# An fp32 kernel with TensorE busy throughout: transposes as pairs of 64-row tiles, and HGRN level scores as 32- and 64-column tiles

## The chip, the cores and the metric

The kernel runs on one core of one Trainium2 chip. The metric is the device time of one execution in microseconds (us). Every time below is in us unless it says ns. The core has five engines that matter here: TensorE (PE; its weight loads are listed apart as PEld), VectorE (DVE), ScalarE (ACT), GpSimd (POOL) and SyncE (SP, which only issues DMAs in this kernel).

## The reference

One inference step of a one-layer hybrid streaming encoder, on a prompt of 512 frames and on a sample of 32 frames that continues running streams. Two branches work in parallel on one projection and are merged by sigmoid gates.

```python
D_MODEL, SEQ, DEC_SEQ, CHUNK = 1024, 512, 32, 64
proj = xn @ w_in                      # u, v_m, z_m, ig, fg, q_h, f_h, i_h, g_h, ga, gb
# branch 1, mLSTM, 4 heads of 512: conv + silu -> q, k; chunked scores; matrix memory C
s = einsum('bhtd,bhsd->bhts', q, k) * dmat
num = w_inter * einsum('bhed,bhtd->bhte', C, q) + einsum('bhts,bhse->bhte', s, v)
# branch 2, HGRN2, 8 heads of 128
g = cumsum(lf)                                         # log forget gates
dec = exp(where(causal, g[t] - g[s], -inf))            # one decay per channel
a = einsum('bhtc,bhtsc,bhsc->bhts', q, dec, k)
o = einsum('bhtc,bhce->bhte', q * exp(g), S) + einsum('bhts,bhse->bhte', a, v)
# head norms, silu gates, y = sigmoid(ga) * ya + sigmoid(gb) * yb, two more projections, final norm
```

The outputs are both streams' frames and both branches' new states.

## The kernel before, in words

All data is held with channels on the 128 partitions and the 544 frames (32 of the sample, then 512 of the prompt) along the free dimension. The big projections are matmuls of 272 columns (names `d`, `q`, `k`, `ya`, `yb`), each in three passes, because an fp32 number is split into a high and a low part of the type fp32r. Pairs of projections (class `Two`) are made from seven products instead of eight, in half units of six passes of 272 columns.

TensorE's order is written out by hand. The list of half units is held by `Pump`; the small work of a branch is a Python generator (`mchain(h, pump)` for mLSTM head h, `chain(h)` for HGRN head h) that says `yield n` where n half units of projections are to be put between two of its steps. On TensorE the two are thus woven together: a few small matmuls, then six to eighteen projection passes, and so on. ACT, DVE and POOL are ordered by a scheduler from priorities, except in the first stage.

The change touches these places:

- Transposes. A `PE.transpose` takes a 128x128 fp32 block as weights and an identity (or `anti`, the reversed identity) of 128 columns as the moving operand. `paux` gives a PSUM tile of two banks. `mchain` transposes keys (`kt`, four blocks per 128 frames, L1122; `kts` for the sample, 96 columns, L1135), values (`vt` L1157, `vts` L1175, heads 1 to 3) and the normed outputs (`yt` L1307, four blocks and one of the sample, L1308). `chain` transposes `kq` to sum a diagonal (`pd`, five blocks, L1871), values and keys (`ht`, five blocks each, L1902 and L1903) and outputs (`hoT`, five blocks, L1975 and L1976).
- HGRN scores. `chain(h)` builds the causal scores of a 128-frame block from seven levels c = 1, 2, 4, ..., 64 (`LEVELS`): at level c the keys of one half of each 2c frames meet the queries of the other half. Per level ACT copies keys into `km` (L1818), TensorE multiplies `km` with `qq`, two 128x128 fp32 products into `pl` (L1832, each in two passes), DVE copies what the level needs into `at` under a mask (`COPY_PREDICATED`, L1857), and DVE multiplies `kk` and `qq` by the level's decays (L1850), after which the next `km` can be copied. At c = 16 two more products serve the sample (L1834, L1836), one of them from `snap`, the sample's keys and queries of four levels side by side.
- Sample products. `su` (states, L1922) and `ho` (outputs, L1948 and L1949) have the sample's 32 frames held as four copies in 128 rows.

Of the kernel before, what the change touches and what calls it, by code (L numbers as in the profile page):

```python
# [17 lines left out]
P = 128  # L18
D = 1024
KD = D // P  # L20
NS = 32
# [15 lines left out]
QUADS = P // NS  # L37
STEPS = (2, 3, 3, 3, 3, 3, 3)
# [29 lines left out]
def hybrid_step(ctx: ExitStack, tc: tile.TileContext, a, o):  # L68
# [45 lines left out]
    def psplit(src, name, ring):  # L114
        hi, lo = pair_tile(name, ring)
        S.copy(hi, src)
        V.tensor_tensor(lo, src, hi.bitcast(F32), ALU.subtract)
        return hi, lo

# [196 lines left out]
    def masks():  # L316

        t = cp.tile([P, T], F32, tag="lm", name="lmask")
        u, n = t[:, :T].bitcast(U8), len(LEVELS) * HB
        return u[:, :n].rearrange("p (l t) -> p l t", l=len(LEVELS)), u[:, n : n + NS]  # L320
# [791 lines left out]
    def mchain(h, pump):  # L1112
# [5 lines left out]
        for b in range(NB):  # L1118
            yield 4 if h else 1
            pt = paux(f"kt{h}{b}")  # L1120
            for f in range(KH):
                PE.transpose(pt[:, 0, f * P : (f + 1) * P], kf[f][:, NS + b * P : NS + (b + 1) * P], ident)  # L1122
            kh, kl = slot(f"kwh{h}{b}", F32R), slot(f"kwl{h}{b}", F32R)
            wc = col[:, 10 + b, h : h + 1]
            with tc.high_priority():
                kh_ = S.mul(kh[:, :HD], pt[:, 0, :], wc)
                kl_ = V.scalar_tensor_tensor(kl[:, :HD], pt[:, 0, :], wc, kh[:, :HD].bitcast(F32), ALU.mult, ALU.subtract)
            kw.append((kh, kl))
            if h == 0 and b == NB - 2:
                with tc.issue_after(kh_.ins), tc.issue_after(kl_.ins):  # L1130
                    sample_values(vsum)
        yield 4 if h else 2
        pt = paux(f"kts{h}")
        for f in range(KH):
            PE.transpose(pt[: 3 * NS, 0, f * P : (f + 1) * P], ksm[:, f], ident)  # L1135
# [3 lines left out]
        with tc.high_priority():  # L1139
            S.mul(kws, pt[: 3 * NS, 0, :], wc)  # L1140
            lo = slice(2 * NS, 3 * NS)
            low = V.scalar_tensor_tensor(kws[lo], pt[lo, 0, :], wc[lo], kws[lo].bitcast(F32), ALU.mult, ALU.subtract)
# [6 lines left out]
        else:  # L1149
# [3 lines left out]
            for b in range(NB):  # L1153
                yield 1
                pt = paux(f"vt{h}{b}")
                for f in range(KH):
                    PE.transpose(pt[:, 0, f * P : (f + 1) * P], vt[f][:, NS + b * P : NS + (b + 1) * P], ident)  # L1157
# [5 lines left out]
                with tc.high_priority():  # L1163
                    S.copy(vh[:, :HD], pt[:, 0, :])
                    V.tensor_tensor(vl[:, :HD], pt[:, 0, :], vh[:, :HD].bitcast(F32), ALU.subtract)
# [8 lines left out]
            for f in range(KH):  # L1174
                PE.transpose(pt[: 3 * NS, 0, f * P : (f + 1) * P], vsm[:, f], ident)  # L1175
            vs = small("vs", [3 * NS, VW], F32R, bufs=1)
            with tc.high_priority():
                S.copy(vs[:, :HD], pt[: 3 * NS, 0, :])
            G.tensor_copy(vs[:, HD:VW], vone)
            lo = slice(NS, 2 * NS)  # L1180
            with tc.high_priority():
                low = V.tensor_tensor(vs[lo, :HD], pt[lo, 0, :], vs[lo, :HD].bitcast(F32), ALU.subtract)
# [116 lines left out]
        for f in range(KH):  # L1299
# [6 lines left out]
            for b in range(NB):  # L1306
                PE.transpose(pt[:, 0, b * P : (b + 1) * P], yb[b][:, f * P : (f + 1) * P], ident)  # L1307
            PE.transpose(pt[:, 1, :P], yb[NB][:, f * P : (f + 1) * P], ident)  # L1308
# [4 lines left out]
            with tc.high_priority():  # L1313
                V.scalar_tensor_tensor(c[:, NS:T], pt[:, 0, :], g, c[:, NS:T], ALU.mult, ALU.add)
                V.scalar_tensor_tensor(c[:, :NS], pt[:, 1, :NS], g, c[:, :NS], ALU.mult, ALU.add)
# [65 lines left out]
    def level_masks():  # L1381
        lmask, smask = masks()
        sxt = small("sxt", [P, P + 2 * NS], bufs=1, tag="vsm")
        nc.sync.dma_start(sxt, a["sxt"])
        for i, c in enumerate(LEVELS):
            V.tensor_scalar(
                lmask[:, i, : 2 * P].rearrange("p (b t) -> p b t", b=2),
                sxt[:, :P].rearrange("p (o t) -> p o t", o=1).to_broadcast([P, 2, P]),
                float(c),
                None,  # L1390
                ALU.is_ge,
            )
        V.tensor_scalar(smask, sxt[:, P : P + NS], 0.5, None, ALU.is_ge)
        V.tensor_scalar(lmask[:, QUADS, 2 * P :], sxt[:, P + NS :], 0.5, None, ALU.is_ge)
        return lmask, smask
# [227 lines left out]
    with tc.manual_schedule(engines={mybir.EngineType.PE}):  # L1623
        for h in range(MH):
# [46 lines left out]
            if h == 0:  # L1671
                with tc.issue_after(last.ins):
                    next(bounds)
                    lmask, smask = level_masks()
# [21 lines left out]
    def units():  # L1696
# [49 lines left out]
        def gate(h, t):  # L1746
            sg = slot(f"sg{h}")
            S.activation(sg[:, :T], t[:, :T], AF.Sigmoid)
            V.tensor_tensor(t[:, :T], t[:, :T], sg[:, :T], ALU.mult)
# [51 lines left out]
    def chain(h):  # L1801

        tf, kk, q0, qq, kq, ii = (hs[h][k] for k in ("tf", "kk", "q0", "qq", "kq", "ii"))
        at = tp.tile([P, NA + P], F32, tag="bc", name=f"at{h}")
        G.memset(at, 0.0)
        snap = small("snap", [P, 2, QUADS, NS], bufs=1, tag="ksm")
# [5 lines left out]
        for li, c in enumerate(LEVELS):  # L1812
            smp = li == QUADS
            n = HB if smp else NA
            km = tp.tile([P, NA], F32, tag="vs", name=f"km{h}{c}", bufs=1)
            pump.behind = held[-1] if held else None
            with tc.high_priority():
# [4 lines left out]
                if li < QUADS:  # L1822
                    S.copy(snap[:, :, li], hs[h]["pair"][:, :, csmp])
# [3 lines left out]
            pn = paux(f"pl{h}{c}")  # L1827
            for b in range(2):
                out, dims = pn[:, 0, b * P : (b + 1) * P], ((2 * c, P // (2 * c)), (HB + c, 2), (1, c))
                if c == 1:  # L1830
                    out, dims = out.rearrange("p (i s) -> p s i", s=2), (dims[1], dims[0])
                PE.matmul(out, km[:, b * P : (b + 1) * P], view(qq, b * P, dims), start=True, stop=True)  # L1832
# [8 lines left out]
            with tc.high_priority():  # L1841
# [15 lines left out]
                V.copy_predicated(at[:, :n], lmask[:, li, :n], pn[:, 0, :n])  # L1857
                if smp:
                    for i in range(QUADS):
                        d = slice(i * NS, (i + 1) * NS)  # L1860
                        V.copy_predicated(at[d, NA:HB], smask[d], pn[d, 1, d])
# [4 lines left out]
            if li == 0:  # L1866
# [3 lines left out]
                for b, c_ in enumerate([c_ for c_, _, _ in chunks] + [slice(NA, NA + P)]):  # L1870
                    PE.transpose(pn[:, b // NB, b % NB * P : (b % NB + 1) * P], kq[:, c_], ident)  # L1871
                with tc.high_priority():
                    V.tensor_reduce(
                        dg, pn.rearrange("p a t -> p (a t)")[:, : 5 * P].rearrange("p (b t) -> p b t", t=P), AX.X, ALU.add
                    )
# [11 lines left out]
        def quads(src, i):  # L1887
            G.tensor_copy(snap[:, i], src[:, csmp].rearrange("p (o t) -> p o t", o=1).to_broadcast([P, QUADS, NS]))
            return snap[:, i].rearrange("p l t -> p (l t)")

        kt, it = kk[:, :NP], ii[:, :NP]
        ov = kq
        osb = small("osb", [P, P])
        kit = small("kit", [P, 2, P], tag="qw")
# [3 lines left out]
        for n, src, dst, dss in ((0, ii, it, its), (2, kk, kt, kts)):  # L1898
            yield n
            pt = paux(f"ht{h}")  # L1900
            for b, (c, _, _) in enumerate(chunks):
                PE.transpose(pt[:, 0, b * P : (b + 1) * P], src[:, c], ident)  # L1902
            PE.transpose(pt[:, 1, :P], quads(src, n // 2), ident)  # L1903
            with tc.high_priority():
                S.copy(dst, pt[:, 0, :])
                if n:
                    S.mul(dss, pt[:, 1, :P], 1.0 / QUADS)
                else:
                    S.copy(dss, pt[:, 1, :P])
            if n == 0:  # L1910
# [3 lines left out]
                S.mul(osb, its, dg[:, 4:5])  # L1914
# [33 lines left out]
        PE.matmul(po[:, 1, :P], at[:, NA:], its, start=True, stop=False)  # L1948
        PE.matmul(po[:, 1, :P], qq[:, NA : NA + P], s0, start=False, stop=True)  # L1949
        with tc.high_priority():  # L1950
            V.tensor_tensor(ov[:, :NP], po[:, 0, :], ov[:, :NP], ALU.add)  # L1951
            V.tensor_tensor(osb, po[:, 1, :P], osb, ALU.add)
        hv, hr = small("hv", [P, 5]), small("hr", [P, 5])
        osq = small("osq", [P, P], bufs=1, tag="vsm")
        for b in range(NB):
            S.activation(osq, ov[:, b * P : (b + 1) * P], AF.Square, accum_out=hv[:, b : b + 1])  # L1956
        S.activation(osq, osb, AF.Square, accum_out=hv[:, NB : NB + 1])
# [9 lines left out]
        V.tensor_scalar(osb, osb, hr[:, NB : NB + 1], None, ALU.mult)  # L1967
        hs[h].update(ov=ov, osb=osb)

    def finish(h):  # L1970
# [3 lines left out]
        for b, (_, _, j) in enumerate(chunks):  # L1974
            PE.transpose(pt[:, 0, b * P : (b + 1) * P], ov[:, b * P : (b + 1) * P], ident if j else anti)  # L1975
        PE.transpose(pt[:, 1, :P], osb, anti)  # L1976
        g = vcol(V_HG + h)
        ob = slot(f"ob{h}")
        V.scalar_tensor_tensor(ob[:, NS:T], pt[:, 0, :], g, gg[:, NS:T], ALU.mult, ALU.mult)
        V.scalar_tensor_tensor(ob[:, :NS], pt[:, 1, P - NS : P], g, gg[:, :NS], ALU.mult, ALU.mult)  # L1980
# [231 lines left out]
def _sxt():  # L2212

    p, t = np.arange(P)[:, None], np.arange(P)[None, :]
    s, q, u = p % NS, p // NS, t[:, :NS]
    band = (s > u) & ((s ^ u) >> q == 1)
    last = (p < NS) & (p > u) & ((p ^ u) >= NS // 2)
    return np.concatenate([p ^ t, band, last], axis=1).astype(np.float32)
# [76 lines left out]
```

## Time and profile before

| | |
|---|---|
| runs | 1103.76, 1104.29, 1106.26 us; median 1104.29 |
| profiled execution, first to last instruction | 1101.5 us |
| PE busy | 1092.4 us, 99%, 8625 passes |
| DVE busy | 922.8 us, 84% |
| ACT busy | 693.1 us, 63% |
| POOL busy | 209.5 us, 19% |
| HGRN stage (627 to 885 us): PE, DVE, ACT busy | 257.33, 248.00, 183.14 of 258 us |

The profiled execution's own total time is not among the times shown; its span lies 2.8 us below the median of the runs, and the rest lies before the first and after the last instruction. In a timeline row the columns are the start, the time that the group's records cover, the engine, the line, the operation, out<-in by the program's names, the weights' rows*columns, the moving operand's shape and the count. A matmul's recorded length holds its latency; what it costs on a full TensorE is the distance from its start to the next one's.

### The profile page before, as it was taken

To read this page: it belongs to the slowest core of one execution; us is meant where nothing else is said; L and a number is where in the kernel's file an instruction comes from. 1 tells how busy PE (TensorE), PEld (TensorE's weight loads), DVE (VectorE), ACT (ScalarE), POOL (GpSimd) and SP (SyncE) were. 2 spreads that over 40 slices of the span, in tenths; PEclk is the share of its full clock that TensorE was granted. 3 is DMA by queue.
4 is the path that set the end of the run, shared out by engine and by line. 5 is a ranking of instruction groups with operands and counts; after the bars stand their busy time and mean duration, and the time that the engine had idled before them with its cause. 6 is when DMAs were issued, how large, how long until landed. Compare 5 with 4: busy or idle time off the path is not lost.

```text
span 1101.5 us, 23773 instructions
## 1 busy us (share of the span) xinstructions
PE 1092.4 (99%) x8625; PEld 1070.9 (97%) x8625; DVE 922.8 (84%) x2103; ACT 693.1 (63%) x1579; POOL 209.5 (19%) x375
## 2 busy tenths in 40 slices
PE   9999999999999999999999999999999999999997
PEld 9899999999999999999999999999999999999997
DVE  7889988686896786986888799999999977778885
ACT  7777557754666554665656476776776666446683
POOL 5204010303022021202120123232232210000002
PEclk9999999999999999999999999999999999999999
DMA  7135415639355276554798665666765683337753
GB/s 241 50 124 157 156 58 185 158 125 220 119 178 179 93 178 176 164 167 146 212 261 254 172 145 141 144 135 152 159 145 150 155 222 103 110 90 242 247 180 121
DMA packets 97262, 176.58 MB, mean 160 GB/s; under 512 B 11284, under 2 KB 18580, under 8 KB 96888
## 3 DMA queue, kind: packets, MB, share of 16 engines
q1 hardware_dynamic: 81072, 141.01, 39.9%
q0 software_dynamic: 15184, 32.93, 16.2%
q8 instruction: 68, 1.11, 0.4%
q10 hardware_dynamic: 888, 1.12, 0.3%
q14 instruction: 50, 0.41, 0.1%
HBM read 150.10 MB, written 41.69 MB: 174 GB/s over the span
## 4 chain that ended last, share of the span: by engine, by line
PE 93%; DMA 3%; DVE 2%; issue 1%; SPq 0%; ACT 0%; POOL 0%; ACTq 0%; POOLq 0%
PE d L608 44%; PE ya L167 9%; PE yb L167 4%; PE q L167 4%; PE k L167 4%; PE C L1077 4%; PE nm L1257 3%; PE sc L1037 2%; PE pl L1832 2%; PE u L291 2%; PE d L460 2%; PE vp L1576 2%; DMA ws<-in_w_in 1%; PE ple L167 1%; PE kt L1122 1%; PE ht L1902 1%
## 5 line engine op out<-in xcount | busy, mean ns | idle before, releaser
L495 POOL DMA_DIRECT2D ws<-in_w_in x46 | 40.2, 875 | 211.3 <-DVE hkq L1850 32.2
L622 ACT COPY t<-d 128x272 f32<-128x272 f32 x153 | 58.0, 379 | 14.0 <-PE d L608 14.0
L1850 DVE TENSOR_TENSOR hkq<-hkq,q 128x288 f32<-128x288 f32 (+1 forms) x96 | 40.7, 431 | 2.6 <-PE pl L1834 1.0
L785 DVE SCALAR_TENSOR_TENSOR cv<-ub,vec,cv 128x547 f32<-128x547 f32 x48 | 37.6, 784 | 1.6 <-ACT cv L780 1.2
L1832 PE MATMUL pl<-hkq,km 128*128 128x128 f32 x224 | 36.2, 283 | 0.6 <-ACT km L1818 0.5
L1818 ACT COPY km<-hkq 128x256 f32<-128x256 f32 x56 | 23.9, 428 | 14.2 <-DVE hkq L1850 5.2
L1832 PEld LDWEIGHTS pl<-hkq,km 128*128 128x128 f32 x224 | 30.3, 189 | 2.0 <-ACT km L1818 1.5
L1191 DVE SCALAR_TENSOR_TENSOR c<-c,wi,Cs 128x258 f32<-128x258 f32 x32 | 15.3, 479 | 18.8 <-PE Cs L1189 18.5
L1354 DVE TENSOR_TENSOR y<-ya,y 128x272 f32<-128x272 f32 x48 | 18.9, 435 | 12.1 <-PE ya L167 10.3
L1089 ACT COPY Co<-C 128x258 f32<-128x258 f32 x30 | 9.8, 378 | 27.3 <-PE C L1077 24.9
L1857 DVE COPY_PREDICATED at<-lmask,pl 128x256 f32<-128x256 uint8 (+1 forms) x56 | 25.2, 451 | 0.1
L777 POOL COPY uo<-ub 128x3 f32<-128x3 f32 x16 | 18.7, 1167 | 34.5 <-DVE ub L631 26.6
L1268 ACT COPY y<-nm 128x516 f32<-128x516 f32 x16 | 9.4, 590 | 23.0 <-PE nm L1257 22.5
L133 POOL TENSOR_TENSOR wple50l<-wple5r,wple50h 128x256 fp32r<-128x256 f32 x1 | 0.7, 736 | 120.9 <-ACT wple50h L132 120.9
L961 POOL COPY ksm<-kf 128x96 f32<-128x96 f32 x16 | 7.1, 445 | 84.9 <-ACT kf L975 84.9
L961 POOL COPY vsm<-vt 128x96 f32<-128x96 f32 x12 | 6.3, 525 | 85.9 <-ACT vt L633 43.5
L1797 POOL TENSOR_SCALAR_AFFINE_SELECT aa<-at 128x128 f32<-128x128 f32 x32 | 19.6, 643 | 8.2 <-DVE at L1857 8.0
L581 POOL DMA_DIRECT2D ws<-in_w_in x14 | 14.6, 1043 | 33.1 <-DVE ws272l L133 27.3
L1245 DVE BATCH_NORM_STATS2 bs<-y 128x6 f32<-128x512 f32 (+1 forms) x20 | 13.8, 692 | 8.3 <-ACT y L1268 8.0
L1257 PE MATMUL nm<-vhl,sh 128*128 128x258 f32 x112 | 18.4, 286 | 0.0
L376 POOL DMA_DIRECT2D w_pg_d<-in_w_pg x16 | 13.1, 818 | 25.1 <-issue 21.4
L1956 ACT ACTIVATE osq<-kq 128x128 f32<-128x128 f32 x32 | 9.8, 305 | 12.4 <-DVE kq L1951 12.1
(4735 smaller groups left out, 5086.7 us busy)
## 6 DMA issues: line engine op xcount, KB each, us to landing
ws<-in_w_in POOLq DMA_DIRECT2D x60, 256.0 KB, 4.9
ws<-in_w_in SPq DMA_DIRECT2D x46, 256.0 KB, 3.9
ya_d<-y SPq DMA_DIRECT2D x32, 272.0 KB, 2.3
y<-ya_d SPq DMA_DIRECT2D x24, 272.0 KB, 3.3
w_out_d<-in_w_out POOLq DMA_DIRECT2D x24, 256.0 KB, 6.5
w_pg_d<-in_w_pg POOLq DMA_DIRECT2D x24, 256.0 KB, 6.5
c<-in_C SPq DMA_DIRECT2D x16, 258.0 KB, 3.8
out_Cs<-c SPq DMA_DIRECT2D x16, 258.0 KB, 3.8
```

The source lines that it names most:

```text
L167: PE.matmul(both[b][:m, :TH], part(w, off + k * step, m, x), xx[:, half(b)], start=(k == 0 and j == 0), stop=(k == n - 1 and j == 2),)
L291: PE.matmul(both[b][:m, :TH], part(w, off + k * step, m, x), xx[:, half(b)], start=(k == 0 and j == 0), stop=(k == KD - 1 and j == 2),)
L495: G.dma_start(t, piece(u, i), accum_op=ALU.add)
L608: PE.matmul(ps, ww[:, c], xx, start=(start and k == 0 and j == 0), stop=end, skip_group_check=not start,)
L622: self.kept = S.copy(t, ps)
L785: V.scalar_tensor_tensor(cv[:, :547], ub[:, j : j + 547], vcol(V_CW + 4 * ft + j), cv[:, :547], ALU.mult, ALU.add)
L1077: PE.matmul(pn[g][:, :VH], kw[b][x][:, f * P : (f + 1) * P], vv[b][y][:, g * VH : (g + 1) * VH], start=(b == 0 and j == 0), stop=(b == NB ...
L1257: PE.matmul(pn[:, g, :VH], st[j][x][:, (i - j) * P : (i - j + 1) * P], vv[j][y][:, g * VH : (g + 1) * VH], start=(j == 0 and q == 0), stop ...
L1818: low = S.copy(km.rearrange("p (n j c) -> p n j c", j=2, c=c), view(kk, HB, ((2 * c, NA // (2 * c)), (c - HB, 2), (1, c))),)
L1832: PE.matmul(out, km[:, b * P : (b + 1) * P], view(qq, b * P, dims), start=True, stop=True)
L1850: V.tensor_tensor(x, x, d, ALU.mult)
L1857: V.copy_predicated(at[:, :n], lmask[:, li, :n], pn[:, 0, :n])
```

## The change

Each transpose becomes two: rows 0 to 63 and rows 64 to 127 of the block, each with a 64-column identity, as TensorE tiles of 64 rows and 128 columns that write the two banks of the PSUM tile. What reads PSUM then reads both banks in one instruction with one more dimension, and where it is a `scalar_tensor_tensor` on `kt`, `kts` or `yt`, in two instructions. The sample's last block of `yt` and `hoT` is transposed alone, as a tile of 32 rows.

The level scores are computed only in the blocks that a level needs: for c up to 32 as eight products of 128 rows, 32 weight columns and 32 moving columns (in four column tiles that write 32 partitions each), for c = 64 as four of 64 by 64. For c below 32 four more 32x32 products compute the sample's scores at every level. The masked copy on DVE is 96 columns wide and done at five levels; c = 32 and c = 64 are copied by ACT (one copy and four small ones; two small ones). `snap` and its copies are gone. The sample's state and output products take 32 rows instead of 128.

```diff
+    def turn(pt, i, src, eye=None):
+        n = src.shape[-1]
+        for r in range(2):
+            k = slice(r * HP, (r + 1) * HP)
+            at_ = ident[k, k] if eye is None else eye[k, P - (r + 1) * HP : P - r * HP]
+            PE.transpose(pt[:n, r, i * HP : (i + 1) * HP], src[k], at_)
+    def turned(pt, n, m=P):
+        return pt[:m, :, : n * HP].rearrange("p r (f c) -> p f r c", f=n)
...
-                PE.transpose(pt[:, 0, f * P : (f + 1) * P], kf[f][:, NS + b * P : NS + (b + 1) * P], ident)
+                turn(pt, f, kf[f][:, NS + b * P : NS + (b + 1) * P])
...
-                PE.transpose(pt[:, 0, b * P : (b + 1) * P], yb[b][:, f * P : (f + 1) * P], ident)
-            PE.transpose(pt[:, 1, :P], yb[NB][:, f * P : (f + 1) * P], ident)
+                turn(pt, b, yb[b][:, f * P : (f + 1) * P])
+            PE.transpose(pt[:, 0, 2 * P : 2 * P + NS], yb[NB][:NS, f * P : (f + 1) * P], ident[:NS, :NS])
...
-                if li < QUADS:
-                    S.copy(snap[:, :, li], hs[h]["pair"][:, :, csmp])
...
+            w = max(c, NS)
             for b in range(2):
-                out, dims = pn[:, 0, b * P : (b + 1) * P], ((2 * c, P // (2 * c)), (HB + c, 2), (1, c))
...
-                PE.matmul(out, km[:, b * P : (b + 1) * P], view(qq, b * P, dims), start=True, stop=True)
-            if smp:
-                PE.matmul(pn[:, 0, NA:HB], kk[:, NA : NA + P], qq[:, csmp], start=True, stop=True)
-                ks, qs = (snap[:, i].rearrange("p l t -> p (l t)") for i in range(2))
-                PE.matmul(pn[:, 1, :P], ks, qs, start=True, stop=True)
+                for g in range(P // w):
+                    key = b * P + g * w
+                    out = pn[g * w : (g + 1) * w, 0, b * w : (b + 1) * w]
...
+                    PE.matmul(out, km[:, key : key + w], ask, start=True, stop=True)
+            if c < NS:
+                for g in range(QUADS):
+                    PE.matmul(
+                        pn[g * NS : (g + 1) * NS, 0, 2 * NS : 3 * NS], kk[:, csmp], qq[:, csmp], start=True, stop=True
+                    )
...
-                V.copy_predicated(at[:, :n], lmask[:, li, :n], pn[:, 0, :n])
...
+                if c < NS:
+                    V.copy_predicated(near, lmask[:, li], pn[:, 0, : 3 * NS])
+                elif c == NS:
+                    S.copy(far, pn[:, 0, : 2 * NS])
+                else:
+                    for g in range(2):
+                        k = slice(g * c, (g + 1) * c)
+                        S.copy(
...
+            if c == NS:
+                for g in range(QUADS):
...
+                    S.copy(at[k, :NA].rearrange("p (b q s t) -> p b q s t", b=2, q=2, s=2)[:, :, g // 2], both_)
...
-        PE.matmul(po[:, 1, :P], at[:, NA:], its, start=True, stop=False)
-        PE.matmul(po[:, 1, :P], qq[:, NA : NA + P], s0, start=False, stop=True)
+        PE.matmul(po[:NS, 1, :P], near[:NS, 2 * NS :], its, start=True, stop=False)
+        PE.matmul(po[:NS, 1, :P], qq[:, csmp], s0, start=False, stop=True)
```

TensorE's order of projections and steps stays as it was; what changes is what stands in a step. In `mchain` of head 0, first block of `yt`, TensorE has before (here `d` is a projection, `y` a normed output of 128 frames; shapes are the moving operand's, and the numbers behind the names tell tiles apart):

```order
L608 MATMUL d_2103<-xfh_1737,wa224l 128x272
L1307 MATMUL yt_2239<-ident,y_1940 128x128
L1307 MATMUL yt_2239<-ident,y_1962 128x128
L1307 MATMUL yt_2239<-ident,y_1991 128x128
L1307 MATMUL yt_2239<-ident,y_2029 128x128
L1308 MATMUL yt_2239<-ident,y_1732 128x128
L608 MATMUL d_2103<-xfh_1755,wa224h 128x272
```

and with the change, in the same place:

```order
L624 MATMUL d_2128<-xfh_1762,wa224l 128x272
L129 MATMUL yt_2264<-ident,y_1965 128x64 x2
L129 MATMUL yt_2264<-ident,y_1987 128x64 x2
L129 MATMUL yt_2264<-ident,y_2016 128x64 x2
L129 MATMUL yt_2264<-ident,y_2054 128x64 x2
L1339 MATMUL yt_2264<-ident,y_1757 128x32
L624 MATMUL d_2128<-xfh_1780,wa224h 128x272
```

Five instructions became nine between the same two projection passes. In `chain(1)` the step of level c = 64 and the transpose of the values behind it stand on TensorE before as

```order
L608 MATMUL d_9598<-xfh_1326,ws374l 128x272
L1832 MATMUL pl_9802<-hkq_8958,km_9772 128x128 x2
L1902 MATMUL ht_9818<-ident,hi_9136 128x128 x4
L1903 MATMUL ht_9818<-ident,snap 128x128
L608 MATMUL d_9836<-xh_714,wa1151h 128x272
```

and with the change as

```order
L624 MATMUL d_9921<-xfh_1326,ws374l 128x272
L1860 MATMUL pl_10163<-hkq_9194,km_10133 64x64 x4
L129 MATMUL ht_10182<-ident,hi_9393 128x64 x10
L624 MATMUL d_10204<-xh_714,wa1151h 128x272
L624 MATMUL d_10204<-xl_715,wa1151h 128x272
```

Two kinds of tile, 64 columns wide and then 64 rows high, now follow each other without a projection between them. ACT's queue ahead of the same step, from `km` of c = 32 to `km` of c = 64, reads before

```order
L1818 COPY km_9730<-hkq_8958 128x256
L1720 ACTIVATE q_9714<-hkq_9364 128x288
L1721 ACTIVATE q_9714<-hkq_9364 128x256
L132 CAST wa2274h<-wi66r_9545 128x512
L622 COPY t_9750<-d_9598 128x272
L132 CAST ws474h<-ws_9389 128x512
L1818 COPY km_9772<-hkq_8958 128x256
```

and with the change

```order
L1841 COPY km_10081<-hkq_9194 128x256
L1746 ACTIVATE q_10060<-hkq_9661 128x256
L149 CAST wa1251h<-wi51r_9825 128x512
L638 COPY t_10101<-d_9921 128x272
L149 CAST wa2274h<-wi66r_9859 128x512
L1889 COPY at_9783<-pl_10115 128x64
L1906 COPY at_9783<-at_9783 32x2x64 x4
L149 CAST ws474h<-ws_9690 128x512
L1841 COPY km_10133<-hkq_9194 128x256
```

The copies out of level 32's product (L1889) and the four that place its blocks (L1906) now stand between the two `km` copies, ahead of the one that level 64 needs.

More of the change, by code (lines that the diff above doesn't have):

```diff
@@ L1134, in mchain @@
         for f in range(KH):
[L1135 removed]
+            turn(pt, f, ksm[:, f])
         kws = small("kws", [3 * NS, HD], F32R, bufs=1)
@@ L1901, in chain @@
             for b, (c, _, _) in enumerate(chunks):
-                PE.transpose(pt[:, 0, b * P : (b + 1) * P], src[:, c], ident)
-            PE.transpose(pt[:, 1, :P], quads(src, n // 2), ident)
+                turn(pt, b, src[:, c])
+            turn(pt, NB, src[:, NA : NA + P])
             with tc.high_priority():
[L1905 to L1909, printed above, removed]
+                S.copy(quarters(dst), turned(pt, NB))
+                S.copy(two(dss), pt[:NS, :, NB * HP : (NB + 1) * HP])
             if n == 0:
```

140 lines of the change are left out of this document (77 added, 63 removed).

## The prediction

> **What bounds the kernel now.** I read the busy shares first, then TensorE's waits, then the timeline of TensorE around each kind of small step. Two lines of the page:
>
> ```profile
> PE 1092.4 (99%) x8625; PEld 1070.9 (97%) x8625; DVE 922.8 (84%) x2103; ACT 693.1 (63%) x1579; POOL 209.5 (19%) x375
> ...
> PE 93%; DMA 3%; DVE 2%; issue 1%; SPq 0%; ACT 0%; POOL 0%; ACTq 0%; POOLq 0%
> ```
>
> TensorE is busy from end to end, and 93% of the chain that ended last is its own. A busy share can hide waits, since records carry latency; but of all that it waited for after its warm-up, the list of waits has this at the top:
>
> ```profile
> PE pl L1832 <- ACT km L1818: 0.5, 1, 0.5
> ```
>
> So TensorE's time is a sum of slots, and the change is worth what it takes from or adds to those slots. DVE and ACT count only where they make TensorE late. The price of a small step is read as the distance from the last projection pass before it to the second one behind it (the first one's start is recorded early), less two projection slots. The timeline of TensorE, for slots and transposes:
>
> ```profile
> 651.50 1.05 PE L1921 MATMUL su<-hi,hkq 128*128 128x128 f32 x8
> 652.39 0.39 PE L1922 MATMUL su<-kit 128*128 128x128 f32 x2
> ...
> 250.19 0.29 PE L608 MATMUL d<-xh,wa1236l 128*128 128x272 f32 x1
> 250.32 0.60 PE L1157 MATMUL vt<-ident,vt 128*128 128x128 f32 x4
> ...
> 250.89 0.29 PE L608 MATMUL d<-xl,wa1236h 128*128 128x272 f32 x1
> ...
> 153.52 0.29 PE L608 MATMUL d<-xfh,wa224l 128*128 128x272 f32 x1
> 153.64 0.60 PE L1307 MATMUL yt<-ident,y 128*128 128x128 f32 x4
> 154.08 0.27 PE L1308 MATMUL yt<-ident,y 128*128 128x128 f32 x1
> ...
> 154.32 0.29 PE L608 MATMUL d<-xfl,wa224h 128*128 128x272 f32 x1
> ```
>
> From the last projection pass to the first start behind it go 0.13, 0.12 and, in the next fence, 0.13: a slot is 0.126. Eight fp32 passes of 128 columns take 0.89, so 0.111 each. Four transposes cost 250.89 - 250.19 - 0.25 = 0.45, five cost 0.80 - 0.25 = 0.55. The same for level steps, at c = 8, c = 16, and c = 64 with the five transposes (`ht`) that follow it:
>
> ```profile
> 637.12 0.29 PE L608 MATMUL d<-xh,wa1273l 128*128 128x272 f32 x1
> 637.25 0.64 PE L1832 MATMUL pl<-hkq,km 128*128 128x128 f32 x4
> ...
> 637.86 0.29 PE L608 MATMUL d<-xfl,wa2249h 128*128 128x272 f32 x1
> ...
> 670.59 0.29 PE L608 MATMUL d<-xh,ws450l 128*128 128x272 f32 x1
> 670.72 0.61 PE L1832 MATMUL pl<-hkq,km 128*128 128x128 f32 x4
> ...
> 671.74 0.29 PE L608 MATMUL d<-xl,ws450h 128*128 128x272 f32 x1
> ...
> 677.74 0.29 PE L608 MATMUL d<-xfh,ws374l 128*128 128x272 f32 x1
> 677.88 0.71 PE L1832 MATMUL pl<-hkq,km 128*128 128x128 f32 x4
> ...
> 679.11 0.29 PE L608 MATMUL d<-xl,wa1151h 128*128 128x272 f32 x1
> ```
>
> They cost 0.74 - 0.25 = 0.49, 1.15 - 0.25 = 0.90, and 1.37 - 0.25 = 1.12.
>
> **What the new tiles cost.** The trace of before already holds fp32 steps in smaller tiles: transposes in 32 rows (`cols`), and products in four 32-column tiles side by side (`vq`, `nm` L1203). `nm` L1204 is an fp32r product and runs like a full tile.
>
> ```profile
> 90.73 0.42 PE L167 MATMUL q<-cs3h,wq001l 128*128 128x272 f32 x2
> 91.08 1.27 PE L916 MATMUL cols<-ident,row 4*128 4x4 f32 x18
> 92.22 0.28 PE L918 MATMUL cols<-ident,r 4*96 4x4 f32 x3
> 92.43 0.52 PE L167 MATMUL q<-cs0h,wq010h 128*128 128x272 f32 x2
> 92.78 0.41 PE L167 MATMUL q<-cs0l,wq010h 128*128 128x272 f32 x2
> ...
> 46.56 0.63 PE L1576 MATMUL vp<-wv3h,x 128*128 128x512 f32 x2
> 47.03 0.40 PE L1576 MATMUL vp<-wv3l,x 128*128 128x512 f32 x1
> 47.36 0.62 PE L1586 MATMUL vq<-wv0r,xg 128*32 128x512 f32 x1
> ...
> 47.38 0.62 PE L1586 MATMUL vq<-wv3r,xg 128*32 128x512 f32 x1
> 47.81 0.59 PE L1586 MATMUL vq<-wv0r,xg 128*32 128x512 f32 x1
> ...
> 48.35 0.72 PE L1576 MATMUL vp<-wv4h,x 128*128 128x512 f32 x2
> 48.91 0.40 PE L1576 MATMUL vp<-wv4l,x 128*128 128x512 f32 x1
> ...
> 118.81 0.31 PE L1204 MATMUL nm<-vs,dss 96*32 96x258 f32 x1
> 119.05 0.64 PE L1203 MATMUL nm<-c,qw 128*32 128x258 f32 x8
> 119.62 0.30 PE L1204 MATMUL nm<-vs,dss 96*32 96x258 f32 x1
> 119.76 0.41 PE L460 MATMUL d<-xh,wi350h 128*128 128x272 f32 x2
> ```
>
> What the reader is to see is time that no column explains. `cols`: 18 passes start 0.063 apart (1.14 / 18), three more at 0.05; that is 1.28, and four slots of `q` are 0.50; 92.78 - 90.73 is 2.05, so 0.27 is left. `vq`: 48.91 - 47.03 = 1.88, less two rounds of 0.43 (47.81 - 47.38) and three `vp` slots of 0.235 (47.03 - 46.56 for two), leaves 0.32. `nm`: 119.76 - 118.81 = 0.95, less two rounds of 258 columns (0.43 x 258 / 512 = 0.22 each) and two slots of L1204 (0.126 x 258 / 272 = 0.12 each), leaves 0.27. In each case TensorE runs empty before the new kind of tile and again behind it, and the first weights cannot be loaded ahead. I take **0.30 for leaving full tiles and coming back**, with 0.27 and 0.33 as ends; and 0.12 for one more change of tile inside a step (119.05 - 118.81, less L1204's own 0.12).
>
> Within a kind of tile work does overlap: the four `vq` tiles start within 0.02, and their streams cost 0.84 ns per column (0.43 for 512), so rounds of 32, 64 and 128 columns cost 0.027, 0.054, 0.108. For a half transpose the stream is 0.054, but its weights are still 128 columns, and `cols` shows such loads 0.063 apart in one row tile. No row shows two row tiles at once. Side by side a pair costs 0.063, one after the other 0.126; I take 0.063, because the column tiles, the nearest row, run side by side.
>
> **The sum.** Groups of four transposes (16 `kt`, 4 `kts`, 12 `vt`, 3 `vts`): 0.30 + 4 x 0.063 = 0.55 against 0.45, 35 x 0.10 = +3.5. Groups of five (8 `pd`, 8 second `ht`): 0.62 against 0.55, +1.1. `yt` and `hoT` end in a 32-row tile: 0.55 + 0.12 for the change + 0.063 for the weights + 0.03 = 0.76 against 0.55, 24 x 0.21 = +5.0. Levels 1, 2, 4, 8: 8 + 4 products of two passes in four tiles are six rounds, 0.30 + 6 x 0.027 = 0.46 against 0.49, 32 x -0.03 = -1.0. Level 16: 0.46 against 0.90, 8 x -0.44 = -3.5. Level 32: four rounds, 0.41 against 0.49, -0.6. Level 64 and the first `ht` share one way out and back: 0.30 + 4 x 0.054 + 0.12 + 5 x 0.063 = 0.95 against 1.12, -1.4. `su`: two passes of 0.111 keep their length and gain a tile change, 8 x 0.30 = +2.4. `ho`: four passes of 0.111 become 0.108 each in two further kinds of tile, 0.30 + 0.12 + 0.43 = 0.85 against 0.45, +3.2.
>
> ACT: at c = 64 `km` has no slack.
>
> ```profile
> L1823 ACT COPY snap<-hkq 128x64 f32<-128x64 f32 x31 | 7.6, 245 | 0.0
> ```
>
> ```profile
> 676.42 0.62 ACT L132 CAST ws474h<-ws 128x512 fp32r<-128x512 f32 x1 [0.95 <-PE d L608]
> 677.42 0.41 ACT L1818 COPY km<-hkq 128x256 f32<-128x256 f32 x1 [0.38 <-DVE hkq L1850]
> ```
>
> It ends at 677.83, and `pl` starts at 677.88. Five copies now stand ahead of it, and they wait for level 32's product; at 0.245 (the nearest copy) they are 1.2, against 1.33 of idle time there. TensorE waits between 0 and 1.2 per chain; I take 0.2, +1.6. The rest costs nothing on TensorE's path: DVE gains 44 short instructions and loses wider masked copies, and ACT loses the `snap` copies, both beside TensorE; if that cover failed, `km` would be late, which is the term just counted. No DMA moves.
>
> The sum is +10.3 on the profiled 1101.5, and I put as much on the median of the runs, 1104.29, which lies 2.8 above that span: **1114.6**. Counted over, the change goes out of full tiles and back 147 times and changes tile 40 times more inside a step; that is 49 us of new cost (44 and 5) against 39 saved.
>
> **Rivals.** *Changing tiles is cheap for these.* If neither the 147 trips nor the 40 changes cost anything, the 49 go away: about 1066. The point from which it decides is a trip of 0.23 (10.3 / 147 = 0.07 less than 0.30). Against it stand three rows of three shapes between 0.27 and 0.33; for it, that none of them is 64 rows high. The Trainium skill (TensorEngine Tiling (Array Packing), Theoretical Speedup) promises up to 2x for a dimension up to 64 and 4x up to 32; that is this rival's rule, and by these rows it holds for the streams alone.
>
> *The two row halves run one after the other.* 356 pairs (140 + 80 + 96 + 40) cost 0.063 more: +22, 1137. For it: the only repeated half-like load, `cols`, came at 0.063 and no faster; against it, `vq`.
>
> *Every short pass has a fixed price.* At `cols`' 0.063 whatever the tile, six rounds of four become 1.5 instead of 0.16, 40 x 1.35 = +54, with the halves in turn some 1190. Against it: four starts within 0.02. The Trainium skill (TensorEngine Tiling (Array Packing), Instruction Overhead) speaks against this change here: about 60 cycles per matmul however few columns. By an estimate from it, 25 ns at the 2.4 GHz it gives elsewhere (TensorE: Matmul & The Clock Gate, Terms), a level of 24 passes would take 0.60 and the sum end near 1135; the starts in `vq` disagree.
>
> **Chances.** Forecast 0.58 (its own range 1108 to 1127: trips of 0.27 to 0.33 move it by 4.4 either way, the wait for `km` by -1.6 to +8). Halves in turn 0.18, fixed price 0.05. Cheap changes 0.13. A trip near 0.23, no change, 0.06. A measurement of this kernel can tell 0.2%, 2.2 us, from no change. So faster 0.13, same 0.06, slower 0.81; the range 1104 to 1140 leaves out the cheap changes and the fixed price.
>
> **What would show it.** In the profile after: from the last projection pass before a `kt` step to the second behind it 0.80 (0.55 + 0.25), not 0.70; the two halves of a pair starting within 0.02, pairs 0.06 apart; the c = 8 step near 0.71; the c = 16 step down to it; an idle stretch of TensorE's loads of about 0.2 ahead of each small tile. A half following the other at 0.06 shows the second rival, a step without the gap the first. It would be wrong if 64-row tiles need no emptying, or if TensorE waits for `km` far more than 0.2.

## The result, and the profile after

The changed kernel takes 1117.97 us (median of four runs, 1117.28 to 1118.82) against 1104.03: a ratio of 1.0124, with an interval of 1.0110 to 1.0138. It is 13.9 us slower; 10.3 were forecast. The profiled executions are 1117.0 and 1101.5 us long, 15.5 apart. In the runs on record a total lies 1.7 to 2.0 above its own span (1118.82 for 1117.0), so of the 2.8 between the span before and its median only about 1.8 lie outside the span. The execution profiled before was some 0.7 below its median, the one after 0.9 above its own; that makes up the difference between 15.5 and 13.9.

The page's busy shares and the chain that ended last, after:

```profile
PE 1107.4 (99%) x9877; PEld 1053.0 (94%) x9877; DVE 914.4 (82%) x2095; ACT 706.4 (63%) x1603; POOL 189.0 (17%) x367
...
PE 90%; ACT 3%; DVE 3%; issue 1%; DMA 1%; SPq 0%; ACTq 0%; DVEq 0%
```

TensorE is still busy from end to end. It issues 1252 more instructions, and its weight loads are busy for less of the span (94% for 97%). The first load of a small step does not run ahead while a projection streams: in the `kt` step below it starts at 233.34, together with its own pass and 0.22 behind the last projection pass.

The small steps, read as in the prediction: from the last projection pass before a step to the second one behind it, less 0.25. TensorE's timeline of the changed kernel, for a `kt` group, a level 4 step, level 16, level 64 with the first `ht`, `su`, and `hoT`:

```profile
233.12 0.29 PE L624 MATMUL d<-xfh,ws320l 128*128 128x272 f32 x1
233.34 0.46 PE L129 MATMUL kt<-ident,kf 64*128 64x64 f32 x8
...
233.96 0.29 PE L624 MATMUL d<-xl,wa1122h 128*128 128x272 f32 x1
...
706.54 0.28 PE L624 MATMUL d<-xh,wa1175l 128*128 128x272 f32 x1
706.75 0.33 PE L1860 MATMUL pl<-hkq,km 128*32 128x32 f32 x16
...
707.31 0.28 PE L624 MATMUL d<-xl,wa1175h 128*128 128x272 f32 x1
...
712.12 0.29 PE L624 MATMUL d<-xh,ws451l 128*128 128x272 f32 x1
712.33 0.33 PE L1860 MATMUL pl<-hkq,km 128*32 128x32 f32 x16
...
712.89 0.29 PE L624 MATMUL d<-xl,ws451h 128*128 128x272 f32 x1
...
719.10 0.29 PE L624 MATMUL d<-xfh,ws375l 128*128 128x272 f32 x1
719.54 0.45 PE L1860 MATMUL pl<-hkq,km 128*64 128x64 f32 x8
...
720.61 0.29 PE L624 MATMUL d<-xl,wa1152h 128*128 128x272 f32 x1
...
724.02 0.29 PE L624 MATMUL d<-xh,wa1252l 128*128 128x272 f32 x1
724.15 1.05 PE L1957 MATMUL su<-hi,hkq 128*128 128x128 f32 x8
725.13 0.48 PE L1958 MATMUL su<-kit 32*128 32x128 f32 x2
...
725.77 0.29 PE L624 MATMUL d<-xfl,wa2275h 128*128 128x272 f32 x1
...
744.82 0.28 PE L624 MATMUL d<-xh,ws452l 128*128 128x272 f32 x1
...
745.43 0.24 PE L2013 MATMUL hoT<-anti,osb 32*128 32x32 f32 x1
...
745.83 0.29 PE L624 MATMUL d<-xfl,ws276h 128*128 128x272 f32 x1
```

They give 0.59 for `kt`, 0.52 for both steps of levels 4 and 16, 1.26 for level 64 with `ht`, 1.50 for `su`, 0.76 for `hoT`. The first small pass starts 0.21 or 0.22 behind the last projection pass (later at level 64, of which more below), where a full tile starts 0.126 behind it. Summed over all steps of each kind, before and after:

| steps | forecast | before, us | after, us | measured |
|---|---|---|---|---|
| 35 groups of four | +3.5 | 15.9 | 20.4 | +4.5 |
| `pd`, second `ht` (16) | +1.1 | 8.8 | 10.4 | +1.6 |
| `yt`, `hoT` but the last | +5.0 | 13.1 | 19.1 | +6.0 |
| levels 1, 2, 4, 8 (32) | -1.0 | 15.5 | 16.8 | +1.2 |
| level 16 (8) | -3.5 | 7.5 | 4.2 | -3.3 |
| level 32 (8) | -0.6 | 3.9 | 3.9 | +0.1 |
| level 64, first `ht`, last `hoT`; `km` late | +0.2 | 10.2 | 10.7 | +0.5 |
| `su` (8) | +2.4 | 8.9 | 12.0 | +3.1 |
| `ho` (8) | +3.2 | 16.1 | 19.5 | +3.4 |

The sum is +17.1. The two profiled executions differ by 15.5; the 1.6 between the two stands outside the small steps. Of that, 1.2 lies behind TensorE's last pass, which ends 6.5 before the end of the span before and 5.4 after; the rest was not traced.

### The profile page after: what moved, and what is told of

It reads as the page before. It is cut to its first block, busy times and chain, and to the rows that moved or that the text cites. A ratio compares the mean times of both kernels' runs of the same rounds, so it can differ in the third digit from the quotient of the medians.

```text
span 1117.0 us, 26333 instructions
## 1 busy us (share of the span) xinstructions
PE 1107.4 (99%) x9877; PEld 1053.0 (94%) x9877; DVE 914.4 (82%) x2095; ACT 706.4 (63%) x1603; POOL 189.0 (17%) x367
## 3 DMA queue, kind: packets, MB, share of 16 engines
q8 instruction: 77, 1.26, 0.5%
q10 hardware_dynamic: 888, 1.12, 0.3%
## 4 chain that ended last, share of the span: by engine, by line
PE 90%; ACT 3%; DVE 3%; issue 1%; DMA 1%; SPq 0%; ACTq 0%; DVEq 0%
PE d L624 42%; PE ya L184 9%; PE yb L184 4%; PE q L184 4%; PE k L184 4%; PE C L1093 4%; PE nm L1288 3%; PE sc L1053 2%; PE u L308 2%; PE d L476 2%; PE vp L1601 2%; PE pl L1860 1%; PE ple L184 1%; ACT at L1906 1%; PE ht L129 1%
## 5 line engine op out<-in xcount | busy, mean ns | idle before, releaser
L638 ACT COPY t<-d 128x272 f32<-128x272 f32 x153 | 58.0, 379 | 15.9 <-PE d L624 15.5
L1860 PEld LDWEIGHTS pl<-hkq,km 128*32 128x32 f32 (+1 forms) x832 | 13.2, 112 | 10.3 <-ACT km L1841 3.5
L1860 PE MATMUL pl<-hkq,km 128*32 128x32 f32 (+1 forms) x832 | 19.7, 204 | 1.3 <-ACT km L1841 0.5
L1822 POOL TENSOR_SCALAR_AFFINE_SELECT aa<-at 128x128 f32<-128x128 f32 x32 | 16.0, 565 | 14.2 <-ACT at L1893 14.2
L392 POOL DMA_DIRECT2D w_pg_d<-in_w_pg x16 | 13.1, 819 | 25.6 <-issue 25.5
L793 POOL COPY uo<-ub 128x3 f32<-128x3 f32 x16 | 10.0, 628 | 42.8 <-DVE ub L647 29.4
L1288 PEld LDWEIGHTS nm<-vhl,sh 128*128 128x128 f32 x112 | 15.4, 190 | 0.5 <-ACT Co L1105 0.5
```

Source lines behind the costliest of these rows:

```text
L638: self.kept = S.copy(t, ps)
L1288: PE.matmul(pn[:, g, :VH], st[j][x][:, (i - j) * P : (i - j + 1) * P], vv[j][y][:, g * VH : (g + 1) * VH], start=(j == 0 and q == 0), stop ...
L1860: PE.matmul(out, km[:, key : key + w], ask, start=True, stop=True)
```

## Experiments

Differences are taken to the median of the kernel before measured beside each run, 1104.0 to 1104.7.

**The two parts alone.** First the transposes alone, in the kernel before; then their opposite, the changed kernel with full transposes in all but the sample's block of `hoT`, which stays a 32-row tile:

```diff
-    PE.transpose(pt[:, 0, f * P : (f + 1) * P], kf[f][:, ...], ident)
+    turn(pt, f, kf[f][:, ...])          # e1: every group; levels, su, ho as before
```

> The kernel before with only the transposes changed (all 91 groups in 64-row halves, the samples of `yt` and `hoT` in a 32-row tile); level scores, `su` and `ho` in full tiles as before. If the cost of the whole change is round trips at the price of the step sum, this part carries most of it: by the prediction's terms +3.5 +1.1 +5.0 = +9.6 and about +0.9 for the first `ht`, which has a trip of its own here, so 1114.5; with the steps as they stand in the profile after (0.59 for four, 0.65 for five, 0.76 with the 32-row tile) about +11.5, so 1115.5. If the cost lay in the scores (small `su` and `ho` tiles, copies ahead of `km`) and the halves were free, within 2 us of 1104.

> The changed kernel with every transpose back in full 128x128 tiles; level scores, `su` and `ho` stay in small tiles. By the step sum: levels 1 to 8 +1.4 (0.52 for 0.48), level 16 -3.0, level 32 0, level 64 alone with its late `km` +1.5, `su` +3.1, `ho` +3.4: about +6, 1110. If the cost of the change lay in the scores, 1116 or more; if the transposes carry all of it, 1104.

(The groups are 83, not 91.) Measured: 1113.5, +9.6 (ratio 1.0087, 1.0072 to 1.0102), and 1109.3, +5.3 (1.0050, 1.0035 to 1.0065). Both parts lose. Together they are 14.9 against the 13.9 of the whole, but a part of the cost of `hoT` stands in both: with four full blocks and the one 32-row tile its step is 0.81 in the second kernel, for 0.55 before, in seven chains, so 1.8 of the 5.3 belong to that tile. The steps alone have the costs that they have in the whole change: `kt` 0.59, `su` 1.50.

**The price of a trip by itself.** A trip is leaving full tiles and coming back to them. Here small tiles that nothing reads stand behind full transposes:

```diff
     # kt: behind the four full transposes
+    PE.transpose(pt[:, 1, :NS], kf[0][:NS, ...], ident[:NS, :NS])
     # vt: four such passes
```

> The kernel before with 28 added trips whose output nothing reads: one 32-row transpose behind each of the 16 `kt` groups, four behind each of the 12 `vt` groups. At the prediction's price a `kt` step becomes 0.30 + 0.06 longer and a `vt` step 0.30 + 4 x 0.063 = 0.55: 16 x 0.36 + 12 x 0.55 = +12.4, 1116.5. At a trip of 0.36 (what the halves' groups leave over their streams in the profile after) +14, 1118. If the cost of the changed kernel is in the halves or in writing two banks and not in leaving full tiles, only the passes remain: 16 x 0.06 + 12 x 0.25 = +4, 1108 or less.

Measured: 1115.8, +11.8 (1.0110, 1.0093 to 1.0127). TensorE's timeline of that kernel, a `kt` and a `vt` step:

```profile
232.13 0.29 PE L608 MATMUL d<-xfh,ws320l 128*128 128x272 f32 x1
232.25 0.60 PE L1122 MATMUL kt<-ident,kf 128*128 128x128 f32 x4
232.78 0.24 PE L1123 MATMUL kt<-ident,kf 32*128 32x32 f32 x1
...
233.19 0.29 PE L608 MATMUL d<-xl,wa1122h 128*128 128x272 f32 x1
...
405.79 0.29 PE L608 MATMUL d<-xh,wa1240l 128*128 128x272 f32 x1
...
406.44 0.43 PE L1160 MATMUL vt<-ident,vt 32*128 32x32 f32 x4
...
407.04 0.29 PE L608 MATMUL d<-xfl,ws340h 128*128 128x272 f32 x1
```

The `kt` step is 0.81, the `vt` step 1.00; both were 0.44. One pass added 0.37, four added 0.56, so a pass costs 0.06 and the way out and back 0.31. The price stands without a half or any changed reader: the forecast's 0.30 holds. The added passes do write the second bank of the PSUM tile, but so do the full tiles of `yt` in the kernel before, where a fifth transpose costs 0.11 like the others. The `hoT` step of the run above, with one 32-row pass in place of a full one, has the same 0.81. A `kt` group of eight halves leaves 0.59 - 0.31 = 0.28 for eight passes of which one alone costs 0.06: they do run in pairs.

**Halves in turn.**

```diff
-    for f in range(KH):
-        turn(pt, f, ...)                # top half, bottom half, next block
+    for r in range(2):                  # all top halves, then all bottom halves
+        for f in range(KH):
+            turn(pt, f, ..., rs=(r,))
```

> The changed kernel with the halves of a group in another order: all top halves first, then all bottom halves, so that neighbours in the order share a row tile. If a pair costs 0.058 because its two halves run side by side, each of the 356 pairs (35 groups of four, 24 of five, 24 of four) now costs 0.058 more: +20.6, 1138.6. If a half is cheap by itself (half the rows, half the load) and nothing runs side by side, no change: 1118. If the two row tiles overlap whatever the order, also 1118, with starts 0.003 apart across the two runs of four.

Measured: 1121.4, 3.4 above the changed kernel. Groups of four hardly changed (`kt` 0.60 for 0.59), groups of five did. TensorE's timeline, `pd`, of this kernel and then of the changed one:

```profile
701.33 0.28 PE L624 MATMUL d<-xfh,ws251l 128*128 128x272 f32 x1
701.54 0.65 PE L129 MATMUL pd<-ident,kq 64*128 64x64 f32 x10
...
702.35 0.29 PE L624 MATMUL d<-xfl,ws251h 128*128 128x272 f32 x1
```

```profile
700.85 0.28 PE L624 MATMUL d<-xfh,ws251l 128*128 128x272 f32 x1
701.06 0.53 PE L129 MATMUL pd<-ident,kq 64*128 64x64 f32 x10
...
701.75 0.28 PE L624 MATMUL d<-xfl,ws251h 128*128 128x272 f32 x1
```

0.77 for 0.65, twice 0.06; 24 such groups make some 2.8 of the 3.4. None of the three expectations gave this. A record does not name its half, so this is read from the starts. In a group of four the first two passes still start within 0.02 of each other, where passes of one half stand 0.06 apart; so one of them is a bottom half, with three top halves between the two in the order. In a group of five, four stand between them, and the starts are four single ones and three pairs: seven slots instead of five. That two halves side by side cost what one costs alone is shown by the difference.

**Fewer trips.**

```diff
-    yield 4 if h else 1
+    yield 0 if b % 2 else (8 if b and h else 4) if h else 1 + b // 2   # vt alike; the yields behind them too
```

> The changed kernel with the `kt` groups and the `vt` groups issued two at a time, with no projection pass between the two: 14 ways out of full tiles and back fewer (8 and 6), the same passes. If the price is paid for each leaving and coming back, 14 x 0.31 (the trip that the added passes gave) and 14 x 0.05 (the longer first pair): -5.0, 1113. If it is paid for each group (its first weights, its two banks), no change: 1118. If the readers of the first group now make the second late, something between.

Measured: 1116.0 (1.0109, 1.0094 to 1.0124), 2.0 below the changed kernel, with intervals that overlap. The steps say more. TensorE's timeline, two `kt` groups together, and the waits of TensorE on the moved groups:

```profile
236.00 0.29 PE L624 MATMUL d<-xfh,wa2220l 128*128 128x272 f32 x1
236.22 0.72 PE L129 MATMUL kt<-ident,kf 64*128 64x64 f32 x16
...
237.10 0.28 PE L624 MATMUL d<-xfl,ws222h 128*128 128x272 f32 x1
```

```profile
PE kt L129 <- DVE kwl L1145: 0.6, 2, 0.3
...
PE vt L129 <- DVE vt L645: 0.4, 1, 0.4
```

A double step is 0.85 where two single ones were 1.18: a trip saved, as expected. Over all `kt` and `vt` steps 3.3 us went, not 14 x 0.33 = 4.6, since two of the double steps waited (1.73 and 1.42 long) for a PSUM reader or for a source that was not ready so early. Even so, a double step only draws level with two full groups, 2 x 0.44.

**The second kind of tile in a step.** The expectation speaks of `yt` and `hoT`; the edit took in `yt` alone, 16 of the 24 groups, so its terms are to be read with two thirds.

```diff
-    PE.transpose(pt[:, 0, 2 * P : 2 * P + NS], yb[NB][:NS, ...], ident[:NS, :NS])
+    turn(pt, NB, yb[NB][:, ...], rs=(0,))
```

> The changed kernel with the sample rows of `yt` and `hoT` in the top 64-row half (one pass, its lower 32 rows unused) and no 32-row tile. If a second kind of tile inside a step costs 0.12 or more, a step falls from 0.76 to 0.59 + 0.06 = 0.65: 24 x 0.11 = -2.6, 1115.3. If only leaving full tiles costs, the pass costs the same in either tile: 1118.

Measured: 1117.5 (1.0123, 1.0108 to 1.0138), not to be told from the changed kernel. TensorE's timeline of a `yt` step:

```profile
158.43 0.29 PE L624 MATMUL d<-xh,ws44l 128*128 128x272 f32 x1
158.65 0.52 PE L129 MATMUL yt<-ident,y 64*128 64x64 f32 x9
...
159.33 0.29 PE L624 MATMUL d<-xl,ws44h 128*128 128x272 f32 x1
```

0.65 for 0.76, as expected; all `yt` steps together fell by 1.6 us.

**The copies ahead of `km`.** In the changed kernel ACT's timeline at level 64 reads:

```profile
717.30 1.23 ACT L1906 COPY at<-at 32x128 f32<-32x128 f32 x4
718.55 0.62 ACT L149 CAST ws475h<-ws 128x512 fp32r<-128x512 f32 x1
719.08 0.40 ACT L1841 COPY km<-hkq 128x256 f32<-128x256 f32 x1
```

`km` ends at 719.48 and `pl` starts at 719.54, 0.43 behind the last projection pass instead of 0.21. The four copies were moved:

```diff
-    S.copy(at[k, :NA].rearrange(...)[:, :, g // 2], both_)
+    G.tensor_copy(at[k, :NA].rearrange(...)[:, :, g // 2], both_)
```

> The changed kernel with the four copies that place level 32's blocks on POOL, away from ACT's row ahead of level 64's `km`. If these copies make `km` late, the step of level 64 with the first `ht` falls from 1.24 to about 1.02: 8 x 0.22 = -1.8, 1116.2. If `km` is late for another reason (DVE's product, ACT's weight casts), no change: 1118. If POOL's copies take so long that the scores are late for `triangle`, slower than 1118.

Measured: 1118.8 (1.0132, 1.0116 to 1.0149), no gain. The step did fall, from 1.24 to 1.03 in most chains, so the copies are what made `km` late; 1.3 us were won there and 1.3 lost at the second `ht` and `su` behind it. Of what was lost, this wait of TensorE is the largest:

```profile
PE su L1957 <- ACT hkq L1944: 0.7, 1, 0.7
```

**Level 16 alone: four versions.** It is the one step that gains clearly, so it was put alone into the kernel before:

```diff
+    for g in range(QUADS):              # c == 16 only; other levels in full tiles
+        d, key = slice(g * NS, (g + 1) * NS), b * P + g * NS
+        PE.matmul(pn[d, 0, key : key + NS], km[:, key : key + NS], ask, ...)
```

> The kernel before with level 16 alone in 128x32 column tiles (eight key tiles, five sample tiles, the blocks copied by nine short masked copies); every other step as before. By the price of a trip (0.31) and six to seven rounds at 0.03: a step of 0.53 for 0.89, 8 x 0.36 = -2.9, 1101.1, the one place where the saved streams pay the trip. If DVE, busy nearly throughout this stage, is made late by eight more short copies, 1104 or more.

Measured: 1122.6, 18.5 slower (1.0168, 1.0153 to 1.0183). The level 16 step did fall, to 0.56. The waits of TensorE, its timeline at level 64, and DVE's timeline there:

```profile
PE ht L1917 <- DVE at L1866: 12.8, 6, 2.1
```

```profile
677.09 0.69 PE L1838 MATMUL pl<-hkq,km 128*128 128x128 f32 x4
679.91 1.09 PE L1917 MATMUL ht<-ident,hi 128*128 128x128 f32 x4 [2.13 <-DVE at L1866]
...
681.46 0.43 PE L608 MATMUL d<-xh,wa1151l 128*128 128x272 f32 x1
681.69 0.43 PE L608 MATMUL d<-xh,wa1151h 128*128 128x272 f32 x1
```

```profile
679.33 0.43 DVE L1866 COPY_PREDICATED at<-lmask,pl 128x256 f32<-128x256 uint8 x1
...
679.87 0.25 DVE L1995 SCALAR_TENSOR_TENSOR ob<-hoT,vec,hg 128x32 f32<-128x32 f32 x1
```

DVE's row, the order of its instructions, is made by a planner from priorities. With other copies in it, the second reader of `hoT` (the 32 columns at 679.87) slid behind level 64's masked copy. In the kernel before it stood ahead of even level 32's, which DVE starts at 676.59:

```profile
675.45 0.25 DVE L1980 SCALAR_TENSOR_TENSOR ob<-hoT,vec,hg 128x32 f32<-128x32 f32 x1
```

So `hoT` kept one of the two PSUM buffers of its ring, and `ht` waited for the other until that copy ended at 679.76. Two versions put the readers of `hoT` back by priority, the second with level 64 and the first `ht` in small tiles as well:

```diff
+    with tc.high_priority():
         V.scalar_tensor_tensor(ob[:, NS:T], pt[:, 0, :], g, gg[:, NS:T], ALU.mult, ALU.mult)
         V.scalar_tensor_tensor(ob[:, :NS], pt[:, 1, P - NS : P], g, gg[:, :NS], ALU.mult, ALU.mult)
```

> The kernel with level 16 alone in column tiles, and the two DVE instructions that read `hoT` given high priority, so that they stand ahead of level 64's masked copy in DVE's row. If the last run was slow because the second of them stood behind that copy and held the PSUM buffer that `ht` needed (TensorE waited 12.8 us there), the waits go and the saved streams remain: 8 x 0.33 = -2.6, 1101.4. If DVE as a whole is too late with eight more short copies, TensorE waits elsewhere for it and the time stays at 1104 or more.

> As the kernel beside it, and level 64 in 128x64 column tiles together with the first `ht` in 64-row halves, which follows at once, so that both share one way out of full tiles and back; their copies stay on DVE as before, so that `km` is not late. The step of level 64 with `ht`, 1.11 before, was 1.03 in the run in which `km` was on time: 8 x 0.08 = -0.6 more, 1100.8. If the price of the second kind of tile eats it, no more than the kernel beside it, 1101.4; if the halves' readers or the added copies make DVE or ACT late, slower.

Measured: 1112.3 and 1113.9 against 1104.7 (1.0063, 1.0049 to 1.0077; 1.0083, 1.0069 to 1.0097). No `ht` waits more than 0.2 any more, so the reader was the cause there; but in three of the eight chains of either version another DVE instruction now came late. The waits of TensorE in the first of the two:

```profile
PE hoT L1991 <- DVE osb L1982: 6.0, 3, 2.0
```

Level 64 with `ht` took 1.03 in most chains of the second, where full tiles beside it took 0.99: the pairing does not pay. The last two differ only in priorities:

```diff
-    V.copy_predicated(at[d, NA:HB], smask[d], pn[d, 1, d])   # four times
+    V.copy_predicated(at[:, NA:HB], smask, pn[:, 1, :NS])    # once; both versions
+    with tc.high_priority():            # only in the second; the two `ob` readers too
         V.tensor_scalar(osb, osb, hr[:, NB : NB + 1], None, ALU.mult)
```

> Level 16 alone in column tiles, as in the first kernel of that kind, but with the four sample blocks of a chain written to the same 32 columns and copied by one masked copy: six short copies on DVE where the kernel before has one wide and four short, nine in the earlier attempts. In the planned row of DVE the second reader of `hoT` now stands ahead of level 64's copy in each chain, as before the change. If the earlier attempts lost by readers that slid behind these copies, TensorE waits for nothing and the saved streams remain: 8 x 0.33 = -2.6, 1101.5. If column tiles at level 16 cost DVE's time whatever its order, 1104 or more.

> As the kernel beside it, with the readers of `hoT` and the scaling of its sample rows given high priority, so that both readers stand ahead of level 16's copies. If the order of DVE's row is all that was lost in the earlier attempts, the same as the kernel beside it, 1101.5; if the readers now make level 16's or level 32's product late, `km` and TensorE wait, and it is slower by what they wait.

Measured: 1113.3 (1.0083, 1.0070 to 1.0095), and 1103.3 (0.9990, 0.9981 to 0.9999) against 1104.4. Ten microseconds apart, with the same instructions on each engine's list: the planned order alone. In the slower one TensorE's projections wait for weights that DVE writes, in six chains, one row each like this; in the better one little but `km` is late, most of all once, when ACT stood 2.75 idle before a cast that waited for its weights' transfer:

```profile
PE d L608 <- DVE wa1151l L133: 1.7, 1, 1.7
```

```profile
PE pl L1838 <- ACT km L1818: 2.7, 5, 1.5
```

The last version is the only one not slower than the kernel before. It is 1.1 us faster, less than the 0.2% that a measurement of this kernel can tell; the step of level 16 saves 8 x 0.34 = 2.7, and TensorE waits 2.7 for `km` where it waited 0.5.

## Why the prediction was right

- *The mechanism.* The sum was made of round trips at 0.30. The run with added passes gives 0.31, and both parts of the change lose about what the sum of their trips and streams says (9.6 where 10.5 to 11.5 were expected, 5.3 where about 6 were). The rival of cheap changes is out, halves one after the other too (a pair costs what one half costs), and so is a fixed price per short pass: the 24 passes of a level take 0.52 - 0.31 = 0.21, below 0.01 each, where the prediction's estimate for this rival was 0.60. (The 2.4 GHz of that estimate stands in the Trainium skill, TensorE: Matmul & The Clock Gate, under What's actually happening, not under Terms.) The sizes fit less well: the terms below make +17.1 where the sum had +10.3.
- *Levels 1 to 8, the term most off* (-1.0 against +1.2). 0.46 a step was forecast from six rounds of 0.027; the rounds take 0.21 instead of 0.16, so 32 steps lie just above break-even, not below. Level 32 was off by about as much a step.
- *Groups of halves* (+3.5 and +1.1 against +4.5 and +1.6). In every group the second pair starts about 0.05 later than the rest. The forecast had every pair at 0.063. The halves of nearly every pair start within 0.01 of each other, as forecast.
- *`yt` and `hoT`* (+5.0 against +6.0). 0.76 was forecast for the step and 0.76 measured. Two `yt` steps, of 1.15 and 1.19, make most of the rest: they wait for DVE's reads of the `yt` before, which are three now and were two, a cost that was put at nothing. From TensorE's waits in the changed kernel:

```profile
PE yt L129 <- DVE c L1348: 0.7, 2, 0.4
```

- *`su`* (+2.4 against +3.1). 0.39 a step instead of 0.30. The forecast let the two passes keep their 0.111, and they did not: the second 32-row pass of 128 columns starts 0.21 behind the first (0.48 recorded for the two, 0.27 for one). Why it does is not shown.
- *`km` late* (+1.6) was right in place and size: 0.22 a chain at level 64. Taking it away gave the time back to the steps behind.
- *Level 64 with the first `ht`* (with `km`, +0.2 against +0.5) came out near partly by luck. With `km` on time the step took 1.03, not the 0.95 of the forecast; but in one chain of the kernel before, TensorE waited there, 1.81 for 1.12, and no step of the changed kernel is that long. Nor is 1.12 the price of the streams alone: in the versions with priorities the same full tiles took 0.99.
- *Level 16* (-3.5 against -3.3) was right, but bringing it home by itself took an order of DVE's row that the change does not contain.

## What to carry to other kernels

A small tile has to pay for leaving full tiles and coming back, here 0.31 us. Count what the step streams before and after: 0.90 against 0.21 at level 16 pays; 0.44 against 0.28 in a group of transposes does not, and two groups together only draw level. And where a planner orders an engine that is nearly full, a changed handful of short instructions can cost more by whom they push behind them than they take: read the row of that engine for late readers of shared buffers.

## What the hardware showed beyond that

- Idle time halves the clock. In the first version of level 16 alone, TensorE's projections stand 0.23 apart after the wait of 2.13, where a slot is 0.126. The windows of that kernel (time, length, busy time of PE, weight loads, DVE, ACT and POOL, then the granted clock):

```profile
676.00:678.00 2.00, 1.78 (x14) 1.55 (x13) 1.90 (x5) 1.51 (x5) 0.89 (x1) 1.00 0.16 8
...
680.00:682.00 2.00, 2.00 (x10) 2.00 (x11) 2.00 (x7) 0.76 (x3) 2.00 (x3) 0.50 0.00 0
```

  Each such stretch is 3.41 long in the trace's clock record, and at 0.23 a slot it adds some 1.5 to the wait: 12.8 of waits and 6 x 1.5 = 9.0 of slow clock, less the 2.7 saved, make 19.1, where 18.5 was measured. In the slower of the last two versions, waits of 1.7 were followed by it in two of six chains. Length is not all that decides: within a run the stretches begin whole multiples of 3.41 apart (34.13 here, 129.71 in the slower of the last two). In the second version with priorities, of three equal waits of 2.0, the two that fell between two marks of such a grid were followed by half speed, and the one that lay across a mark was not. But two of the four waits of 1.7 that were not followed by it also fell between two marks, so what decides stays open. The Trainium skill (TensorE: Matmul & The Clock Gate, Why this matters for your kernels) warns of gaps above about 3 us; here waits of 2.0 to 2.1 were enough in eleven of twelve cases.
- By its starts, a pass of the other row tile runs ahead of its turn in the order, past three waiting passes but not past four (`kt` 0.60 for 0.59, `pd` 0.77 for 0.65).
- The Trainium skill's factors of 2 and 4 (TensorEngine Tiling (Array Packing), Theoretical Speedup) are nearly reached here by the streams (0.111 for a full transpose, 0.06 for a pair of halves; 0.48 for level 32 in full tiles, 0.46 - 0.31 = 0.15 in column tiles), not by the steps around them.
